# Gates and branch projections of a hybrid decoder layer: tokens as weights, 512 weight columns moving

## The chip, the cores and the metric

One core of a Trainium2 chip runs the whole layer in one launch. The metric is the device time of one execution in microseconds (us); less is better. TensorE (PE) multiplies matrices into PSUM, VectorE (DVE) and ScalarE (ACT) do the elementwise work, GpSimd (POOL) sets up masks and starts some DMAs, and the queue of SyncE (SP) starts nearly all DMAs.

## The reference

A residual layer over 256 tokens of width 2048 (one layer, batch 1):

```python
h = rms_norm(x, norm_w)
proj = h @ w_in                       # 2048 x 16592
(g_qkv, g_z, g_b, g_a, r_feat, r_z, s_u, s_z, gate_logits) = split(proj)
o_a = gdn_branch(...)                 # gated DeltaNet, width 1024
o_b = rwkv7_branch(...)               # RWKV-7 time mixing, width 1024
o_c = s5_branch(...)                  # diagonal SSM, GLU, times silu(s_z), width 1024
branch_proj = o_i @ w_branch[i]       # for o_a, o_b, o_c: 3 x (256 x 2048)
gates = sigmoid(gate_logits + gate_b) # 3 x (256 x 2048)
merged = sum(gates * branch_proj)
out = rms_norm(x + merged @ w_out, final_norm_w)
```

The three gates take 6144 of the 16592 columns of `w_in`. Everything is float32.

## The kernel before, in words

**Matmuls.** Each float32 product is made of three matmuls in the `float32r` type: both operands are split into a high and a low part, and high x high, high x low and low x high are added up in PSUM (names `whi`, `wlo` for weights, `hT`, `oT`, `mT` pairs for activations). `hT` is the normalised input turned, channels on partitions and 256 tokens in a row.

**Jobs and units.** The weights are read as a stream of units of 128 x 1024 numbers. `load_unit` issues the DMA (`raw`, 4 buffers), ACT makes `whi` (L267), DVE makes `wlo` (L268), 3 buffers each. `run_stream` loads two units ahead of the one that `mm_unit` multiplies. There are two sorts of job:

- `job_cols`: 128 weight columns are the stationary operand, the 256 tokens move. 16 steps (2048 channels) or 8 (1024), three matmuls of 128x256 each. The result has columns on partitions. A unit holds 8 steps.
- `job_tok`: 128 tokens are the stationary operand, up to 512 weight columns move. The result has tokens on partitions, one PSUM bank for each half of the tokens (`a` = 0, 1). A unit with 512 columns holds 2 steps, 12 matmuls. Before, only the output projection (`last`) used it.

**Order.** PE works in the order in which the program is written (class `InOrder`). The other engines are ordered by the scheduler of the framework, as tiles become ready. Other work is woven into the stream by hand: generators lie in lanes, and each call of `pump` is one turn; a generator that yields n is resumed n turns later. `mm_unit` calls `pump` after every second step of a `job_cols`, `run_stream` after every unit; so a turn is six matmuls, four turns a unit. `finish` runs lanes to their end.

**Stages.** 1: `front`, the inputs of DeltaNet and RWKV with their recurrences in lanes. 2: `front_gates`, six gate jobs (`NG` = 6 gate tiles are kept). 3: `front_su`, the input of S5. Then the right-hand pool `fp` closes, and `mp`, `s5p` and `sp` open on the right. 4: `back1`, the other 26 gate jobs of branches 0 and 1, their 32 projections, then six of the eight jobs of S5's gate (`sz_job`); S5 runs in lanes "s" and "sm" the while (`s5_setup`, `s5_mats`, `s5_tile`, eight tiles). The first step of `s5_setup` loads three parameters (`s5raw`, `s5ldt`), yields 1, and turns them on PE (tile `s5t`). 5: `back2`, two more `sz_job`, the GLU of S5, and gates and projections of branch 2. 6: `last`, the output projection and the final norm.

**Gate and projection before.** `gate_job(b, n)` makes 128 columns of gate b, `got_gate` applies tanh(x/2 + b/2) with the bias as ACT's per-partition operand (`hgate`). `proj_job(b, n)` makes the same 128 columns of a branch's projection from `oT[b]`; `got_proj` adds (tanh + 1) * projection to `merged` (columns on partitions, as the output projection wants it) and, with the third branch, splits it into `mT`. The PSUM pool `ps` has two banks for `mm` and six for `br` (everything else).

Of the kernel before, what the change touches and what calls it, by code (L numbers as in the profile page):

```python
# [18 lines left out]
P = 128  # L19
T = 256  # L20
# [16 lines left out]
def tile_trunk(  # L37
# [36 lines left out]
    st_o = ExitStack()  # L74
    op_ = st_o.enter_context(tc.tile_pool(name="op", bufs=1))
    dp = ctx.enter_context(tc.tile_pool(name="dp", bufs=2, space=bass.MemoryType.DRAM))
    ps = ctx.enter_context(tc.tile_pool(name="ps", bufs=1, space=PSUM))

    NB_MM, NB_BR = 2, 6

    def mm_bank(name):
        return ps.tile([P, 512], F32, tag="mm", bufs=NB_MM, name=name)

    def br_bank(name):
        return ps.tile([P, 512], F32, tag="br", bufs=NB_BR, name=name)
# [268 lines left out]

    gmask = cp.tile([P, 2, 64], F32, name="gmask")
    ge.memset(gmask, 1.0)

    lmask = cp.tile([P, 64], F32, name="lmask")
    ge.memset(lmask, 1.0)
    for h in range(2):  # L360
        sl = slice(64 * h, 64 * h + 64)
        select(gmask[sl, 0], ALU.is_gt, 0.0, 0, -1, [[1, 64]])
        select(gmask[sl, 1], ALU.is_ge, 0.0, 0, -1, [[1, 64]])
        select(lmask[sl], ALU.is_gt, 0.0, 0, 1, [[-1, 64]])
    ones = cp.tile([P, 1], F32, name="ones")
    ve.memset(ones, 1.0)
    blk2 = scr[:, 7, 0:P].rearrange("p (a b) -> p a b", a=2)
# [21 lines left out]
    for gi, g in enumerate(groups):  # L389
        rows, eng = pvr[gi], nc.sync  # L390
        if gi == 0:
            ge.memset(rows, 0.0)
        r0 = 0
        for name, src, n in g:
            if n == 0:
                eng.dma_start(out=rows[r0:r0 + 1, 0:96], in_=src.rearrange("(a c) -> a c", a=1))
                n = 1
            else:
                eng.dma_start(out=rows[r0:r0 + n, :], in_=src.rearrange("(a c) -> a c", c=P))
            pv_cols[name] = (gi, r0)  # L400
            r0 += n
        pvt.append((cp.tile([P, r0], F32, name=f"pv{gi}"), r0))

    def pv(name, i=0, n=1):
        gi, r0 = pv_cols[name]
# [6 lines left out]
    nkk = cp.tile([P, 8], F32, name="nkk")  # L412
    hw0 = cp.tile([P, 16], F32, name="hw0")
    hgb = cp.tile([P, 8], F32, name="hgb")
    hgate = cp.tile([P, 48], F32, name="hgate")
    hgnw = cp.tile([P, 1], F32, name="hgnw")
    hlw = cp.tile([P, 16], F32, name="hlw")
    hkk = cp.tile([P, 8], F32, name="hkk")
# [2 lines left out]
    ve.memset(cst[:, 0:1], -RW_C)  # L421
    ve.memset(cst[:, 1:2], EPS)

    def parameters():
        for gi, (t, n) in enumerate(pvt):
            pt = br_bank(f"pvps{gi}")
            pe.transpose(pt[:, 0:n], pvr[gi][:n], ident[:n, :n])
            ve.tensor_copy(t, pt[:, 0:n])
        ve.tensor_scalar(out=omu, in0=pv("mu", 0, 24), scalar1=-1.0, scalar2=1.0, op0=ALU.mult, op1=ALU.add)
        ve.tensor_scalar(out=omu2, in0=pv("mu_wl", 0, 2), scalar1=-1.0, scalar2=1.0, op0=ALU.mult, op1=ALU.add)  # L430
        ve.tensor_scalar(out=nkk, in0=pv("kk", 0, 8), scalar1=-1.0, scalar2=None, op0=ALU.mult)
        ve.tensor_scalar(out=oka, in0=pv("ka", 0, 8), scalar1=-0.5, scalar2=1.0, op0=ALU.mult, op1=ALU.add)
# [4 lines left out]
        ve.tensor_scalar(out=hgate, in0=pv("gate", 0, 48), scalar1=0.5, scalar2=None, op0=ALU.mult)  # L437
# [662 lines left out]
    def lane(name, gen):  # L1100
        lanes.setdefault(name, deque()).append(gen)
# [27 lines left out]
    def mm_unit(u):  # L1129
        job = u["job"]  # L1130
        if u["k0"] == 0:
            job["ps"] = [(br_bank if job["nps"] > 1 else mm_bank)(f"mm{un[0]}_{j}") for j in range(job["nps"])]
        kt, w, k0 = u["kt"], u["w"], u["k0"]
        last = k0 + kt == job["K"]
        mh, ml = job["mov"]()
        if job["tok"]:
# [5 lines left out]
            for a, v in todo:  # L1142
                o = job["ps"][a]
                for k in range(kt):
                    kk = v["k0"] + k
                    end = kk == job["K"] - 1
                    mhs, mls = mh[:, kk, a * P:(a + 1) * P], ml[:, kk, a * P:(a + 1) * P]
                    pe.matmul(o[:, 0:w], lhsT=mhs, rhs=v["hi"][:, k], start=kk == 0, stop=False)
                    pe.matmul(o[:, 0:w], lhsT=mhs, rhs=v["lo"][:, k], start=False, stop=False)
                    pe.matmul(o[:, 0:w], lhsT=mls, rhs=v["hi"][:, k], start=False, stop=end)  # L1150
                if end:
                    job["done"](a, o)
        else:
# [14 lines left out]
            if "after" in job:  # L1168
                job["after"]()

    def job_tok(mat, c, w, done, mov, late=False):
        job = {"K": KD, "tok": True, "nps": 2, "done": done, "mov": mov, "late": late}
        kt = UN // w
        for k0 in range(0, KD, kt):
# [61 lines left out]
    merged = []  # L1236
    gates = {}

    def got_gate(b, i):
        def f(pss):  # L1240
            t = gp.tile([P, T], F32, tag="gate", bufs=NG, name=f"gate{b}_{i}")
            se.activation(out=t, in_=pss[0][:, 0:T], func=AF.Tanh, scale=0.5, bias=hgate[:, b * 16 + i:b * 16 + i + 1])  # L1242
            gates[(b, i)] = t
        return f

    def got_proj(b, i):
        def f(pss):
            g, m, p0 = gates.pop((b, i)), merged[0][:, i], pss[0][:, 0:T]
            if b == 0:
                ve.scalar_tensor_tensor(out=m, in0=g, scalar=1.0, in1=p0, op0=ALU.add, op1=ALU.mult)  # L1250
                return
            ve.scalar_tensor_tensor(out=g, in0=g, scalar=1.0, in1=p0, op0=ALU.add, op1=ALU.mult)  # L1252
            ve.tensor_tensor(out=m, in0=m, in1=g, op=ALU.add)
            if b == 2:
                split(mT[0][:, i], mT[1][:, i], m)
        return f

    def gate_job(b, n):
        return job_cols(W, [(C_GATE + 2048 * b + P * n, P)], got_gate(b, n), hmov)

    def proj_job(b, n):
        return job_cols(w_branch[0, b], [(P * n, P)], got_proj(b, n), lambda: oT[b], K=8)

    NG = 6

    def front_gates():
        for i in range(NG):
            yield from gate_job(i % 2, i // 2)

    run_stream(front(), q=first)  # L1270
    run_stream(front_gates())
    finish("r")
    run_stream(front_su())
    finish("g", "r", "t", "i", "g2", "r2")
    fr.close()

    mp = ctx.enter_context(tc.tile_pool(name="mp", bufs=1, side="right"))
    merged.append(mp.tile([P, KD, T], F32, name="merged"))

    st_s5 = ExitStack()  # L1280
    s5p = st_s5.enter_context(tc.tile_pool(name="s5p", bufs=1, side="right"))
# [26 lines left out]
    def s5_setup(sp):  # L1308
# [2 lines left out]
        nc.sync.dma_start(out=raw[:, 1], in_=s5_a_im[0].rearrange("(i g) n -> i (g n)", g=2))  # L1311
        ldt = sp.tile([32, 2], F32, name="s5ldt")
        nc.sync.dma_start(out=ldt, in_=s5_log_dt[0].rearrange("(i g) -> i g", g=2))
        yield 1
        ve.tensor_copy(raw[:, 2].rearrange("p (g n) -> p g n", g=2), ldt.unsqueeze(2).to_broadcast([32, 2, 64]))
        pt = br_bank("s5t")
        for j in range(3):
# [295 lines left out]
            yield from s5_tile(t)  # L1613

    def back1():
        for n in range(16):
            for b in range(2):
                if (b, n) not in gates:
                    yield from gate_job(b, n)
                yield from proj_job(b, n)  # L1620

    sz = {}
    N_SZ = 6

    def got_sz(i):
        def f(pss):
            p0 = pss[0][:, 0:T]
            th = mp.tile([P, T], F32, tag="szt", name=f"szt{i}")
            se.activation(out=th, in_=p0, func=AF.Tanh, scale=0.5)
            if i < N_SZ // 2:  # L1630
                sz[i] = mp.tile([P, T], F32, tag="sz", bufs=N_SZ // 2, name=f"sz{i}")
            else:
                sz[i] = gp.tile([P, T], F32, tag="gate", bufs=NG, name=f"sz{i}")
            ve.scalar_tensor_tensor(out=sz[i], in0=th, scalar=1.0, in1=p0, op0=ALU.add, op1=ALU.mult)
        return f

    def sz_job(r):
        return job_cols(W, [(C_SZ + P * r, P)], got_sz(r), hmov)
# [121 lines left out]
```

## Time and profile before

| | |
|---|---|
| median of 3 runs | 1197.18 us (1196.2 to 1198.06) |
| the profiled execution | 1195.4 us, span 1193.6 us |
| granted TensorE clock, mean | 0.995 of full |
| busy: PE, PE's weight loads | 1168.8 us, 1128.4 us |
| busy: DVE, ACT, POOL | 905.6 us, 681.6 us, 56.2 us |
| HBM read, mean | 195.88 MB, 169 GB/s over the span |

The span runs from the first to the last instruction of the profiled execution; its time has 1.8 us around that. In the rows shown later, `out<-in` are the program's tile names, then the shapes; "xN | a, b | c" stands for N instructions, a us busy in all, b ns for one on average, c us of idle time of the engine just before them, followed by what ended that idle time. Rows of the timeline begin with the start in us and the length in us of a merged group. Matmuls overlap on PE, so the distance from start to start is their pace, and "mean ns of one" is longer. A row of the chain of waits gives start, length, engine, tile and line.

### The profile page before, as it was taken

Reading aid. Unit: us, or ns where it says so; the run is one execution under the profiler, and the core shown is the slowest. Engines: PE = TensorE matmul, PEld = TensorE weight load, DVE = VectorE, ACT = ScalarE, POOL = GpSimd, SP = SyncE. Lnnn points to the kernel's source line nnn. Section 1 sums busy time; section 2 is a strip of 40 time slices with the busy share of each in tenths; the row PEclk is TensorE's granted clock in tenths of the full one; section 3 lists DMA queues with packets and bytes.
Section 4 is the critical chain, followed back from the end, with each engine's and each line's share of the span. In section 5 each row is a group of like instructions: output and inputs, shape, how many; then the busy total and the mean of one; then the engine's idle time right before and its main releaser. Section 6 shows DMA issues by size and latency. Waiting matters only on the chain. (4 is left out here: it accounts for less than half of the span.)

```text
span 1193.6 us, 29078 instructions
## 1 busy us (share of the span) xinstructions
PE 1168.8 (98%) x11534; PEld 1128.4 (95%) x11534; DVE 905.6 (76%) x2261; ACT 681.6 (57%) x1412; POOL 56.2 (5%) x92
## 2 busy tenths in 40 slices
PE   7999999999999999999989999999999999999997
PEld 7999999999999999999989999999999999999887
DVE  7879696879787888885569979999986665555555
ACT  5465767676767776766534555555544544444443
POOL 1000000000000000000020111111000000000000
PEclk9999999999999999999989999999999999999999
DMA  7766555555656555555657677777776666667763
GB/s 203 195 180 171 153 139 148 141 149 147 159 130 158 148 141 131 132 149 144 182 157 191 181 189 188 195 190 191 185 185 169 182 189 179 188 183 239 242 197 116
DMA packets 384642, 203.97 MB, mean 171 GB/s; under 512 B 38825, under 2 KB 376186, under 8 KB 384122
## 3 DMA queue, kind: packets, MB, share of 16 engines
q1 hardware_dynamic: 382650, 199.61, 62.1%
q0 software_dynamic: 1536, 1.58, 0.6%
q8 instruction: 91, 1.49, 0.5%
q10 hardware_dynamic: 320, 0.93, 0.2%
q14 instruction: 45, 0.37, 0.1%
HBM read 195.88 MB, written 6.18 MB: 169 GB/s over the span
## 5 line engine op out<-in xcount | busy, mean ns | idle before, releaser
L62 PE MATMUL mm<-hT,whi 128*128 128x256 f32 (+1 forms) x4160 | 782.1, 288 | 0.0
L62 PEld LDWEIGHTS mm<-hT,whi 128*128 128x128 f32 (+1 forms) x4160 | 644.6, 191 | 7.3 <-issue 1.2
L62 PE MATMUL mm<-hT,wlo 128*128 128x256 f32 (+1 forms) x2080 | 587.4, 282 | 0.0
L268 DVE TENSOR_TENSOR wlo<-raw,whi 128x1024 fp32r<-128x1024 f32 (+1 forms) x346 | 422.3, 1221 | 184.7 <-ACT whi L267 181.6
L267 ACT ACTIVATE whi<-raw 128x1024 fp32r<-128x1024 f32 (+1 forms) x346 | 365.2, 1056 | 320.2 <-PE mm L62 239.3
L62 PEld LDWEIGHTS mm<-hT,wlo 128*128 128x128 f32 (+1 forms) x2080 | 396.4, 191 | 0.0
L62 PE MATMUL mm<-oT,whi 128*128 128x256 f32 x768 | 142.8, 286 | 0.0
L62 PEld LDWEIGHTS mm<-oT,whi 128*128 128x128 f32 x768 | 120.9, 194 | 0.5 <-issue 0.4
L62 PE MATMUL mm<-oT,wlo 128*128 128x256 f32 x384 | 109.3, 285 | 0.0
L62 PE MATMUL mm<-whi,mT 128*128 128x512 f32 (+1 forms) x288 | 76.8, 354 | 0.0
L62 PEld LDWEIGHTS mm<-oT,wlo 128*128 128x128 f32 x384 | 74.2, 193 | 0.0
L62 PEld LDWEIGHTS mm<-whi,mT 128*128 128x128 f32 x288 | 51.2, 189 | 7.5
L62 PE MATMUL mm<-wlo,mT 128*128 128x512 f32 (+1 forms) x144 | 50.9, 354 | 0.0
L570 DVE TENSOR_TENSOR ivp<-ivZ,ivX 48x1 f32<-48x1 f32 (+14 forms) x120 | 34.6, 288 | 2.0
L688 DVE SCALAR_TENSOR_TENSOR scr<-mm,pv,scr 128x255 f32<-128x255 f32 (+2 forms) x72 | 34.1, 473 | 0.6
L62 PEld LDWEIGHTS mm<-wlo,mT 128*128 128x128 f32 x144 | 27.2, 189 | 3.8
L572 DVE TENSOR_REDUCE ivZ<-ivp 48x1 f32<-48x1 f32 (+14 forms) x120 | 27.3, 227 | 1.7
L62 PE MATMUL mm<-ysp,whi 128*128 128x256 f32 x128 | 23.1, 283 | 0.0
L1252 DVE SCALAR_TENSOR_TENSOR gate<-gate,mm 128x256 f32<-128x256 f32 x32 | 13.3, 417 | 12.1 <-PE mm L62 11.9
L1242 ACT ACTIVATE gate<-mm,hgate 128x256 f32<-128x256 f32 x48 | 22.1, 461 | 0.3
L691 ACT ACTIVATE gth<-scr 128x256 f32<-128x256 f32 x24 | 9.9, 414 | 21.4 <-DVE scr L688 17.8
L62 PEld LDWEIGHTS mm<-ysp,whi 128*128 128x128 f32 x128 | 19.8, 189 | 0.0
(541 smaller groups left out, 1278.4 us busy)
## 6 DMA issues: line engine op xcount, KB each, us to landing
raw<-in_w_in_dram SPq DMA_DIRECT2D x256, 512.0 KB
raw<-in_w_branch_dram SPq DMA_DIRECT2D x48, 512.0 KB
raw<-in_w_out_dram SPq DMA_DIRECT2D x32, 512.0 KB
raw<-in_s_glu_w_dram SPq DMA_DIRECT2D x8, 512.0 KB
xs<-in_x_dram SPq DMA_DIRECT2D x4, 512.0 KB
xr<-in_x_dram SPq DMA_DIRECT2D x2, 1024.0 KB
raw<-in_w_in_dram SPq DMA_DIRECT2D x4, 384.0 KB
gr<-grow SPq DMA_DIRECT2D x8, 128.0 KB
```

What stands on the lines that cost most here:

```text
L62: return self.put(nc.tensor.matmul(*a, **k).ins)
L267: u["top"] = lambda: se.activation(out=hi[:, 0:nn], in_=raw[:, 0:nn], func=AF.Copy)
L268: u["sub"] = lambda eng=ve: eng.tensor_tensor(out=lo[:, 0:nn], in0=raw[:, 0:nn], in1=hi[:, 0:nn].bitcast(F32), op=ALU.subtract)
L570: ve.tensor_tensor(out=pi, in0=Z[:, 0:i, 0:i].rearrange("p j c -> p c j"), in1=X[:, i, 0:i].unsqueeze(1).to_broadcast([8 * NU, i, i]), op= ...
L572: ve.tensor_reduce(out=Z[:, i, 0:i], in_=pi, axis=AX.X, op=ALU.add)
L688: ve.scalar_tensor_tensor(out=c[:, s:T], in0=p[:, 0:T - s], scalar=pv("cw", (3 - s) * 24 + col), in1=c[:, s:T], op0=ALU.mult, op1=ALU.add)
L691: se.activation(out=th, in_=c, func=AF.Tanh, scale=0.5)
L1242: se.activation(out=t, in_=pss[0][:, 0:T], func=AF.Tanh, scale=0.5, bias=hgate[:, b * 16 + i:b * 16 + i + 1])
L1252: ve.scalar_tensor_tensor(out=g, in0=g, scalar=1.0, in1=p0, op0=ALU.add, op1=ALU.mult)
```

## The change

Gates and branch projections become `job_tok` jobs: 128 tokens stationary, 512 weight columns moving. 12 gate jobs instead of 48, 12 projections instead of 48. With that come:

- The gate's bias differs along the row now. It is split into a high and a low part at the start (`parameters`), written to DRAM (`bD`), and for each gate job loaded into rows 0, 1, 64 and 65 of a 128x512 tile that is otherwise zero (`brow`, two of them in turn, set to zero when `mp` opens). A matmul with `blk` (ones in the two diagonal blocks of 64x64) as weights starts each of the two banks with the bias.
- `merged` has tokens on partitions, 128 x 2 x 2048. A new lane "m" (`turn`) turns it with PE transposes after each projection of branch 2, two column blocks (four transposes) at a time, and splits the result into `mT`. What is left of the last one runs inside the first output job.
- Six `sz_job` go to the front in place of six gate jobs. `back1` is then gate and projection of branches 0 and 1 four times, one `sz_job` and the first gate of branch 2.
- `mm_unit` calls `pump` between the steps of a `job_tok` too, three times a unit of 512 columns; a turn is then three matmuls of 512.
- After the front the PSUM pool is closed and opened anew (`ps2`) with four `mm` banks and four `br` banks; `job_tok` takes `mm` banks.
- `s5_setup` yields 8 instead of 1 between its loads and the transposes of `s5t`.

```diff
@@ pools
+    st_ps = ExitStack()
+    banks = [st_ps.enter_context(tc.tile_pool(name="ps", bufs=1, space=PSUM)), 2]
     def mm_bank(name):
-        return ps.tile([P, 512], F32, tag="mm", bufs=NB_MM, name=name)
+        return banks[0].tile([P, 512], F32, tag="mm", bufs=banks[1], name=name)
     def br_bank(name):
-        return ps.tile([P, 512], F32, tag="br", bufs=NB_BR, name=name)
+        return banks[0].tile([P, 512], F32, tag="br", bufs=8 - banks[1], name=name)
...
+    bD = dp.tile([2, 3 * D], F32, tag="bD", bufs=1, name="bD")
     def parameters():
+        bh, bl = (sc3[0:48, (4 + e) * P:(5 + e) * P].bitcast(F32R) for e in range(2))
+        split(bh, bl, pvr[2][0:48])
+        for e, b in enumerate((bh, bl)):
+            nc.sync.dma_start(out=bD[e].rearrange("(a c) -> a c", c=P), in_=b.bitcast(F32))
...
@@ mm_unit
-            job["ps"] = [(br_bank if job["nps"] > 1 else mm_bank)(f"mm{un[0]}_{j}") for j in range(job["nps"])]
+            b_ = mm_bank if job["nps"] == 1 or job["tok"] else br_bank
+            job["ps"] = [b_(f"mm{un[0]}_{j}") for j in range(job["nps"])]
+            if "bias" in job:
+                for o in job["ps"]:
+                    pe.matmul(o, lhsT=blk, rhs=job["bias"].bitcast(F32R), start=True, stop=False)
...
+                    if "pre" in job and a == 0:
+                        job["pre"](kk)
-                    pe.matmul(o[:, 0:w], lhsT=mhs, rhs=v["hi"][:, k], start=kk == 0, stop=False)
+                    pe.matmul(o[:, 0:w], lhsT=mhs, rhs=v["hi"][:, k], start=kk == 0 and "bias" not in job, stop=False)
                     pe.matmul(o[:, 0:w], lhsT=mhs, rhs=v["lo"][:, k], start=False, stop=False)
                     pe.matmul(o[:, 0:w], lhsT=mls, rhs=v["hi"][:, k], start=False, stop=end)
+                    if not job["late"] and (a, k) != (1, kt - 1):
+                        pump()
...
+    NW = 512
+    brow = []
+    def got_gate(b, n):
+        gates[(b, n)] = mp.tile([P, 2, NW], F32, tag="gate", name=f"gate{b}_{n}")
+        def f(a, p):
+            se.activation(out=gates[(b, n)][:, a], in_=p, func=AF.Tanh, scale=0.5)
+        return f
+    def got_proj(b, n):
+        def f(a, p):
+            g, m = gates[(b, n)][:, a], merged[0][:, a, n * NW:(n + 1) * NW]
+            if b == 0:
+                ve.scalar_tensor_tensor(out=m, in0=g, scalar=1.0, in1=p, op0=ALU.add, op1=ALU.mult)
+                return
+            ve.scalar_tensor_tensor(out=g, in0=g, scalar=1.0, in1=p, op0=ALU.add, op1=ALU.mult)
+            ve.tensor_tensor(out=m, in0=m, in1=g, op=ALU.add)
+            if b == 2 and a:
+                lane("m", turn(n))
+        return f
+    def turn(n):
+        yield 4
+        for i in range(4 * n, 4 * n + 4, 2):
+            pt = br_bank(f"mt{i}")
+            for j in range(2):
+                for a in range(2):
+                    pe.transpose(pt[:, (2 * j + a) * P:(2 * j + a + 1) * P],
+                                 merged[0][:, a, (i + j) * P:(i + j + 1) * P], ident)
+            split(*(m[:, i:i + 2].rearrange("p k t -> p (k t)") for m in mT), pt)
+            yield 2
+    def gate_job(b, n):
+        t = brow[(4 * b + n) % 2]
+        for h in range(2):
+            nc.sync.dma_start(out=t[64 * h:64 * h + 2], in_=bD[:, b * D + n * NW:b * D + (n + 1) * NW])
+        return job_tok(W, C_GATE + D * b + NW * n, NW, got_gate(b, n), hmov, bias=t)
+    def proj_job(b, n):
+        return job_tok(w_branch[0, b], NW * n, NW, got_proj(b, n), lambda: oT[b], K=8)
...
     run_stream(front(), q=first)
-    run_stream(front_gates())
+    run_stream(front_sz())
     finish("r")
     run_stream(front_su())
     finish("g", "r", "t", "i", "g2", "r2")
     fr.close()
+    st_ps.close()
+    banks[:] = ctx.enter_context(tc.tile_pool(name="ps2", bufs=1, space=PSUM)), 4
     mp = ctx.enter_context(tc.tile_pool(name="mp", bufs=1, side="right"))
-    merged.append(mp.tile([P, KD, T], F32, name="merged"))
+    merged.append(mp.tile([P, 2, D], F32, name="merged"))
+    for i in range(2):
+        brow.append(mp.tile([P, NW], F32, name=f"brow{i}"))
+        ve.memset(brow[i], 0.0)
...
@@ s5_setup
-        yield 1
+        yield 8
...
     def back1():
-        for n in range(16):
+        for n in range(4):
             for b in range(2):
-                if (b, n) not in gates:
-                    yield from gate_job(b, n)
+                yield from gate_job(b, n)
                 yield from proj_job(b, n)
+        yield from sz_job(6)
+        yield from gate_job(2, 0)
...
     def back2():
-        for r in range(N_SZ, 8):
-            yield from sz_job(r)
+        yield from sz_job(7)
         for r in range(8):
             yield from job_cols(s5_glu_w[0], [(P * r, P)], got_glu(r), lambda: ysp, K=8)
-        for n in range(16):
-            yield from gate_job(2, n)
+        for n in range(4):
+            if n:
+                yield from gate_job(2, n)
             yield from proj_job(2, n)
...
     def last():
-            yield from job_tok(w_out[0], ocut[n], ocut[n + 1] - ocut[n], got_out(n), lambda: mT, late=n == NO - 1)
+            yield from job_tok(w_out[0], ocut[n], ocut[n + 1] - ocut[n], got_out(n), lambda: mT, late=n == NO - 1,
+                               **({} if n else {"pre": lambda k: k == 10 and finish("m")}))
```

More of the change, by code (lines that the diff above doesn't have):

```diff
@@ L76, in tile_trunk @@
     dp = ctx.enter_context(tc.tile_pool(name="dp", bufs=2, space=bass.MemoryType.DRAM))
-    ps = ctx.enter_context(tc.tile_pool(name="ps", bufs=1, space=PSUM))
-    NB_MM, NB_BR = 2, 6
+    st_ps = ExitStack()
+    banks = [st_ps.enter_context(tc.tile_pool(name="ps", bufs=1, space=PSUM)), 2]
     def mm_bank(name):
-        return ps.tile([P, 512], F32, tag="mm", bufs=NB_MM, name=name)
+        return banks[0].tile([P, 512], F32, tag="mm", bufs=banks[1], name=name)
     def br_bank(name):
-        return ps.tile([P, 512], F32, tag="br", bufs=NB_BR, name=name)
+        return banks[0].tile([P, 512], F32, tag="br", bufs=8 - banks[1], name=name)
     UN = 1024
@@ L356, in tile_trunk @@
     ge.memset(gmask, 1.0)
-    lmask = cp.tile([P, 64], F32, name="lmask")
-    ge.memset(lmask, 1.0)
     for h in range(2):
@@ L363, in tile_trunk @@
         select(gmask[sl, 1], ALU.is_ge, 0.0, 0, -1, [[1, 64]])
-        select(lmask[sl], ALU.is_gt, 0.0, 0, 1, [[-1, 64]])
     ones = cp.tile([P, 1], F32, name="ones")
@@ L401, in tile_trunk @@
             r0 += n
-        pvt.append((cp.tile([P, r0], F32, name=f"pv{gi}"), r0))
+        if gi < 2:
+            pvt.append((cp.tile([P, r0], F32, name=f"pv{gi}"), r0))
     def pv(name, i=0, n=1):
@@ L414, in tile_trunk @@
     hgb = cp.tile([P, 8], F32, name="hgb")
-    hgate = cp.tile([P, 48], F32, name="hgate")
     hgnw = cp.tile([P, 1], F32, name="hgnw")
@@ L436, in parameters @@
         ve.tensor_scalar(out=hgb, in0=pv("gb", 0, 8), scalar1=0.5, scalar2=None, op0=ALU.mult)
-        ve.tensor_scalar(out=hgate, in0=pv("gate", 0, 48), scalar1=0.5, scalar2=None, op0=ALU.mult)
         ve.tensor_scalar(out=hgnw, in0=pv("gnw"), scalar1=0.5, scalar2=None, op0=ALU.mult)
@@ L1169, in mm_unit, with job_tok @@
                 job["after"]()
-    def job_tok(mat, c, w, done, mov, late=False):
-        job = {"K": KD, "tok": True, "nps": 2, "done": done, "mov": mov, "late": late}
+    def job_tok(mat, c, w, done, mov, late=False, K=KD, **more):
+        job = {"K": K, "tok": True, "nps": 2, "done": done, "mov": mov, "late": late, **more}
         kt = UN // w
-        for k0 in range(0, KD, kt):
+        for k0 in range(0, K, kt):
             u = {"job": job, "k0": k0, "kt": kt, "w": w, "src": [(0, w, mat[k0 * P:(k0 + kt) * P, c:c + w])]}
@@ L1237, in tile_trunk @@
     gates = {}
-    def got_gate(b, i):
-        def f(pss):
-            t = gp.tile([P, T], F32, tag="gate", bufs=NG, name=f"gate{b}_{i}")
-            se.activation(out=t, in_=pss[0][:, 0:T], func=AF.Tanh, scale=0.5, bias=hgate[:, b * 16 + i:b * 16 + i + 1])
-            gates[(b, i)] = t
-        return f
[L1246 to L1268, printed above, removed]
+    NW = 512
[5 more added lines that the diff above has]
+        return f
@@ new lines, in proj_job, with got_sz @@
+    def proj_job(b, n):
+        return job_tok(w_branch[0, b], NW * n, NW, got_proj(b, n), lambda: oT[b], K=8)
+    sz = {}
+    N_SZ = 6
+    def got_sz(i):
+        def f(pss):
+            p0 = pss[0][:, 0:T]
+            th = ft([P, T], "gth", f"szt{i}") if i < N_SZ else mp.tile([P, T], F32, tag="szt", name=f"szt{i}")
+            se.activation(out=th, in_=p0, func=AF.Tanh, scale=0.5)
+            if i < N_SZ:
+                sz[i] = gp.tile([P, T], F32, name=f"sz{i}")
+            else:
+                sz[i] = mp.tile([P, T], F32, name=f"sz{i}")
+            ve.scalar_tensor_tensor(out=sz[i], in0=th, scalar=1.0, in1=p0, op0=ALU.add, op1=ALU.mult)
+        return f
@@ L1270, in tile_trunk, with sz_job, front_sz @@
+    def sz_job(r):
+        return job_cols(W, [(C_SZ + P * r, P)], got_sz(r), hmov)
+    def front_sz():
+        for i in range(N_SZ):
+            yield from sz_job(i)
     run_stream(front(), q=first)
-    run_stream(front_gates())
+    run_stream(front_sz())
     finish("r")
@@ L1615, in back1 @@
     def back1():
-        for n in range(16):
+        for n in range(4):
             for b in range(2):
-                if (b, n) not in gates:
-                    yield from gate_job(b, n)
+                yield from gate_job(b, n)
                 yield from proj_job(b, n)
[L1622 to L1638, printed above, removed]
+        yield from sz_job(6)
+        yield from gate_job(2, 0)
     lane("s", s5_all())
     run_stream(back1())
-    run_stream(job for r in range(N_SZ) for job in sz_job(r))
     finish("s", "sm")
```

## The prediction

> **What bounds the kernel now.** I read the page first, then the chain of waits, the groups of instructions, and the timeline where the chain has a hole.
>
> ```profile
> PE 1168.8 (98%) x11534; PEld 1128.4 (95%) x11534; DVE 905.6 (76%) x2261; ACT 681.6 (57%) x1412; POOL 56.2 (5%) x92
> ...
> PEclk9999999999999999999989999999999999999999
> ```
>
> PE is busy for 98% of the span and its granted clock dips in one slice alone, the 21st (597 to 627 us). In the chain, in order of time, I looked for what is not PE's matmuls:
>
> ```profile
> 617.21 0.69 PE s5t L65 x3
> 617.89 57.28 PE mm L62 x456
> 675.18 0.44 PE s5bt L65 x4
> ...
> 676.55 15.11 PE mm L62 x126
> ```
>
> It is S5's few transposes, and the hole ahead of s5t, which the dip of the clock goes with. So the time follows the number of PE instructions times their pace, plus that hole. The pace with 256 moving columns is 15.11 us / 126 = 119.9 ns a matmul.
>
> ```profile
> L62 PE MATMUL mm<-hT,wlo 128*128 128x256 f32 x2048 | 578.4, 282 | 0.0
> L62 PE MATMUL mm<-oT,wlo 128*128 128x256 f32 x384 | 109.3, 285 | 0.0
> 1100.59 0.61 PE L62 MATMUL mm<-whi,mT 128*128 128x512 f32 x2
> ...
> 1134.59 0.61 PE L62 MATMUL mm<-whi,mT 128*128 128x512 f32 x2
> ```
>
> The first two rows (groups by form) give the counts: 2048 low-part matmuls are 128 jobs of 16, 384 are 48 jobs of 8, and each step has three matmuls. The last two (timeline) are the output projection, which already has tokens as weights and 512 columns moving. Between them lie 50 triples (each two whi matmuls and one wlo): 34.00 us / 150 = 226.7 ns. Two matmuls of 256 cost 239.8 ns, one of 512 costs 226.7: about 13 ns per instruction do not scale with the columns, and they are what the change can save.
>
> **Pace.** Gates: 48 jobs x 16 x 3 = 2304 matmuls; projections: 48 x 8 x 3 = 1152. Together 3456 x 119.9 ns = 414.4 us. After: the same columns in 1728 matmuls of 512 (12 gate jobs of 96, 12 projections of 48), 391.7 us at the pace of the output projection, whose operands have the same kinds and shapes. Gain 22.7 us. All of it is on PE's path.
>
> **Bias by a matmul.** Two more matmuls of 512 for each of 12 gate jobs: 24 x 226.7 ns = 5.4 us added on PE. The ACT bias operand that they replace cost PE nothing.
>
> **Turning the merged sum.** 32 transposes of 128x128. The row of s5bt has four such in 0.44 us, so 32 x 0.11 = 3.5 us added. The columns' splits become eight of 512 on ACT and DVE, in stages where neither is full.
>
> Sum on PE: -22.7 + 5.4 + 3.5 = -13.8 us.
>
> The Trainium skill, "TensorE: Matmul & The Clock Gate", section "Back-to-back issue gap", gives an isolated matmul N/2.4 + 2.5 ns at full clock, so only some 2.5 ns that halving the count could save: 1728 x 2.5 = 4.3 us, less than 24 x 215.8 ns for the biases and 32 x 55.8 ns for the turns (7.0 us), a loss of 2.7 us for these parts by an estimate from that page. The trace does not agree: 119.9 and 226.7 ns here, where it would give 109.2 and 215.8.
>
> **The hole at the change of stage.** Here the change says that S5's set-up turns later. The timeline around it, all engines:
>
> ```profile
> 595.50 3.47 SPq L264 DMA_DIRECT2D raw<-in_w_branch_dram  x2
> ...
> 612.34 0.40 PE L62 MATMUL mm<-oT,whi 128*128 128x256 f32 x2
> ...
> 613.41 0.43 DVE L105 TENSOR_TENSOR oT<-rog,oT 128x256 fp32r<-128x256 f32 x1 [0.48 <-ACT oT L104]
> 614.00 0.09 DVE L1419 MEMSET cb<- 128x32 f32 x1 [0.16 <-DVE oT L105]
> 614.04 0.31 POOL L1296 MEMSET B<- 128x256 f32 x1 [107.05 <-DVE oT L105]
> 614.12 0.37 SPq L1310 DMA_DIRECT2D s5raw<-in_s_a_re_dram  x1
> 615.01 0.45 SPq L1313 DMA_DIRECT2D s5ldt<-in_s_log_dt_dram  x1
> ...
> 617.21 0.69 PE L65 MATMUL s5t<-ident,s5raw 32*128 32x32 f32 x3 [3.99 <-DMA uD<-us]
> 617.31 0.22 DVE L1315 COPY s5raw<-s5ldt 32x128 f32<-32x128 f32 x1 [1.46 <-DMA s5ldt<-in_s_log_dt_dram]
> ...
> 618.63 0.63 PE L62 MATMUL mm<-oT,whi 128*128 128x256 f32 x2
> ...
> 622.47 0.55 PE L62 MATMUL mm<-oT,whi 128*128 128x256 f32 x2
> ...
> L548 DVE MEMSET Mr<- 128x512 f32 x2 | 1.0, 485 | 0.1
> ```
>
> DVE, POOL and SP all first touch the tiles of the new pools between 614.00 and 614.12, right after the last reader of the old right-hand pool (613.41 + 0.43). So whatever lies in a pool opened there waits until 614.0. PE ran six matmuls of the first projection, then stood at s5t, whose loads were issued at 614.12 to 615.01 and were there at 617.2 (2.3 us from the issue of s5ldt to the copy that waited for it). Lost: 617.89 - 612.34, less six matmuls (0.72) and three transposes at full speed (0.33), is 4.5 us. After it PE is slow: from 618.63 to 622.47 six triples take 3.84 us, 213 ns a matmul; against 119.9 that loses 2.1 us from 617.89 to 622.47. Hole and after-effect cost 6.6 us.
>
> The change lets seven turns pass ahead of s5t, 21 matmuls or 4.8 us: s5t no longer waits. But the stage now begins with a gate, and the first instruction of a gate is the bias matmul. It reads brow, a tile in mp, which opens at the same 614.0. Ahead of it lie a memset of 128x512 (485 ns), then two loads on SP's queue, 0.43 us apart, then the 2.3 us. If they go first: 614.0 + 0.5 + 0.45 + 2.3 = 617.3. If SP has s5's two or three loads out first, because those need no memset, up to 618.1. PE has nothing else: its order is fixed, and every matmul of the stage is queued behind the bias. It stops at 612.34 and loses 5.0 to 5.8 us; I take 5.4, 0.9 more than before. The new PSUM pool also has to wait, for the last copy out of the old banks, which ends sooner and so is under it. The slow 5 us after it remain. Ends: -6.6 (no wait left) and +1.3.
>
> The same page of the Trainium skill, section "HAM oscillation", has a gap of PE over about 3.4 us put the array back to half clock. The 3.99 us hole and the 213 ns agree; by it the new hole would have to fall under 3.4 us before the 2.1 us came back.
>
> **DVE in the S5 stage.**
>
> ```profile
> 500.00:600.00 100.00, 98.83 (x1055) 95.31 (x1055) 63.93 (x163) 62.27 (x151) 1.22 (x1) 1.00 0.57 149
> 727.25:754.50 27.25, 27.25 (x326) 26.55 (x326) 25.61 (x57) 13.79 (x28) 3.65 (x6) 1.00 0.69 182
> ...
> 743.17 0.42 DVE L1581 TENSOR_TENSOR s5s<-s5m,s5m 128x256 f32<-128x256 f32 x1
> 745.23 0.97 PE L62 MATMUL s5y<-s5s,CX 128*32 128x64 f32 x56
> ...
> L1253 DVE TENSOR_TENSOR merged<-merged,gate 128x256 f32<-128x256 f32 x32 | 13.5, 421 | 0.7
> L1702 DVE SCALAR_TENSOR_TENSOR xr<-mm,xr 128x512 f32<-128x512 f32 x6 | 3.8, 682 | 0.0
> L268 DVE TENSOR_TENSOR wlo<-raw,whi 128x1024 fp32r<-128x1024 f32 x342 | 418.2, 1224 | 184.7 <-ACT whi L267 181.6 <-DMA UM<-uD 0.6
> ```
>
> The second row is one S5 tile (columns: stretch, its length, busy PE, PEld, DVE, ACT, POOL, clock, DMA): 33 turns of six matmuls, DVE busy 25.61 of 27.25 us. A turn shrinks from 0.72 to 0.68 us, so a tile to 25.9 us. The merge of two branches falls from 12 instructions of 0.42 per 512 columns to 6 of 0.68; a tile's 198 matmuls are 1.4 of four such column blocks, so that takes 0.3 us off it: DVE 25.3 of 25.9. It fits, barely. The tightest spot is s5s to s5y: done at 743.59, used at 745.23, 1.6 us spare. From s5u to s5y are 21 turns, so 0.84 is lost. The merge now comes in lumps: a projection of the second branch ends in 4 x 0.68 = 2.7 us of DVE at once, every 96 turns. Counted in turns, two of the eight tiles have such a lump inside this stretch (3 x 0.42 before): late by 0.84 + 1.5 - 1.6 = 0.7 us each. I take +0.7 in all, with ends 0 and 5.4 (all eight). The four br banks hold s5bt, two s5u and s5ct at once, just enough. S5 then ends at turn 372 of 424 instead of 365 of 384, well covered.
>
> **The turn's own wait.** The transposes come three turns, nine matmuls or 2.0 us, after the last matmul of proj(2,n). DVE needs two instructions of 0.68 after that; a split of 1.22 in between makes them late by up to 0.7. Four times: 0 to 2.8, I take 0.7. The last turn lies under the first output job, which needs its columns only at the twelfth of 16 steps.
>
> **At nothing.** Six S5-gate jobs for six merge-gate jobs in front: same matmuls, and DVE has room there (64% from 500 to 600 us, first row above). Each gate's two brow loads go to SP ahead of that gate's weights; they wait for a bias matmul two gates back, long done, so they hold up neither the weights nor S5's loads behind them. The first projection's weights were issued at 595.50 for 612.34, so such loads have 17 us of lead; without it each would cost up to 2.3 us. The bD writes, brow's repeated loads and 2 KB instead of 512-byte rows are under PE. The start loses a transpose and gains a small split: 0 to 0.5.
>
> **Sum.** -13.8 + 0.9 + 0.7 + 0.7 = -11.5 us. The profiled execution took 1195.4 us (span 1193.6), so 1183.9; the median of the runs, 1197.18, stands 1.8 above it: 1185.7.
>
> **The rivals.**
> *The hole closes too.* If brow were not held up by the old pool, 4.5 + 2.1 us come back: 1197.2 - 13.8 - 6.6 + 1.4 = 1178.2. Against it: three engines that start at 614.0 together.
> *DVE late, in part.* All eight tiles late by 0.7 and every turn late: 1197.2 - 13.8 + 0.9 + 5.4 + 2.8 = 1192.5.
> *DVE becomes the bound (the other side).* Place: s5s ahead of s5y. If three more splits of 1.22 stand in front of the last s5s in each tile, s5y is late by 3.7 + 0.84 - 1.6 = 2.9 us, eight times: 1197.2 - 13.8 + 0.9 + 0.7 + 23 = 1208. It decides from 1.8 us a tile on (14 us over eight). For it: 94% busy in that tile's row. Against it: DVE's total falls.
> *The pace does not come.* If a 512 matmul costs two of 256 in these stages, -11.5 + 22.7: 1208. Against it: 50 even triples at 226.7. The gap rule of the Trainium skill, weighed above, speaks for a milder form of it.
> *Bias late at every gate.* Eleven more waits of up to 2.3 us: 1211. Against it: the lead of 17 us.
>
> **Chances.** Forecast 0.62 (own range 1182 to 1189). Hole closed 0.13. DVE late in part 0.11. DVE the bound 0.09, of which 0.04 ends within 0.2%. Pace 0.02, bias 0.03. About 0.2%, 2.4 us, is what a measurement of this kernel can tell. Faster 0.86, same 0.04, slower 0.10. The range 1178 to 1191.5 reaches to the closed hole and most of the partial case, leaving out some 2 in 10.
>
> **What will show it.** mm<-whi,hT and mm<-whi,oT of 512 at 680 ns a triple; 24 matmuls reading brow and blk; the first of them with 4.5 to 6 us of idle time before it, released by a DMA, and triples near twice the time after it; s5t without a wait; gaps ahead of s5y of under 1 us in two tiles and ahead of mt of under 1 us. It is wrong if no idle time stands before the first bias, if s5y waits in every tile, or if the triples are slower than 0.70.

## The result, and the profile after

The changed kernel takes 1187.74 us (median of 4 runs, 1186.22 to 1189.48), the kernel before beside it 1196.69 (4 runs): ratio 0.9929, 95% interval 0.9913 to 0.9944, 9.0 us faster. The forecast was 1185.7. The profiled execution is the slowest of the four, 1189.48 us.

The head of its page:

```profile
span 1187.6 us, 25599 instructions
...
PE 1160.4 (98%) x9861; PEld 1045.8 (88%) x9861; DVE 898.2 (76%) x2214; ACT 674.9 (57%) x1381; POOL 55.6 (5%) x89
...
PEclk9999999999999999999999999999999999999998
```

PE is still the bound. It has 1673 instructions fewer (11534 before), and loading weights leaves room: 88% of the span, not 95%. Next the groups by form, the matmuls that are new here:

```profile
L62 PE MATMUL mm<-whi,hT 128*128 128x512 f32 x768 | 246.7, 395 | 0.0
L62 PE MATMUL mm<-wlo,hT 128*128 128x512 f32 x384 | 150.8, 393 | 0.6 <-DVE wlo L267 0.5
...
L62 PE MATMUL mm<-brow,blk 128*128 128x512 f32 x24 | 8.0, 415 | 3.9 <-DMA s5raw<-in_s_a_im_dram 3.9
...
L65 PE MATMUL mt<-ident,merged 128*128 128x128 f32 x32 | 4.9, 274 | 0.0
```

The 24 bias matmuls hold the stage's one large idle time, and the 32 transposes of the merged sum have none ahead of them. The timeline of all engines at the change of stage, where the hole of the kernel before was:

```profile
615.02 0.28 PE L62 MATMUL mm<-hT,wlo 128*128 128x256 f32 x1
...
615.84 0.42 DVE L104 TENSOR_TENSOR oT<-rog,oT 128x256 fp32r<-128x256 f32 x1 [0.48 <-ACT oT L103]
...
616.50 1.02 DVE L1327 MEMSET brow<- 128x512 f32 x2 [0.24 <-DVE oT L104]
616.54 0.37 SPq L1359 DMA_DIRECT2D s5raw<-in_s_a_re_dram  x1
...
617.02 0.55 SPq L1285 DMA_DIRECT2D brow<-bD  x2
...
619.16 1.19 PE L62 MATMUL mm<-brow,blk 128*128 128x512 f32 x2 [3.86 <-DMA s5raw<-in_s_a_im_dram]
...
621.00 1.05 PE L62 MATMUL mm<-whi,hT 128*128 128x512 f32 x2
...
622.28 1.06 PE L62 MATMUL mm<-whi,hT 128*128 128x512 f32 x2
...
626.40 0.62 PE L62 MATMUL mm<-whi,hT 128*128 128x512 f32 x2
...
627.08 0.62 PE L62 MATMUL mm<-whi,hT 128*128 128x512 f32 x2
...
628.08 0.37 PE L65 MATMUL s5t<-ident,s5raw 32*128 32x32 f32 x3
```

Front's last matmul starts at 615.02 and is over at 615.14, counted at its pace of 0.12 us; PE stands until 619.16, 4.0 us. Then a triple takes 1.28 us (621.00 to 622.28; the granted clock from 620 to 625 is 0.50), and 0.68 from about 625 on. 22 matmuls from 619.16 to 627.08 take 7.92 us, at 226.7 ns they would take 4.99: 2.9 lost. So the hole costs 6.9 us, and s5t stands in it no more: no idle time ahead of it at 628.08. The profile puts the wait down to the DMA that landed last, s5raw, which the bias matmul doesn't read; brow's loads went out between those of s5raw.

In S5's stage, the chain of waits (first and last s5y) and the windows:

```profile
721.68 1.47 PE s5y L62 x72
...
908.76 1.47 PE s5y L62 x72
```

```profile
700.00:800.00 100.00, 98.89 (x797) 79.45 (x796) 90.67 (x186) 52.67 (x103) 13.06 (x22) 1.00 0.65 187
800.00:900.00 100.00, 99.57 (x875) 79.68 (x874) 91.96 (x195) 49.03 (x92) 7.28 (x12) 1.00 0.67 194
```

```profile
PE s5y L62 <- DVE s5s L1629: 0.9, 2, 0.6
...
PE mm L62 <- DVE wlo L267: 0.5, 1, 0.5
```

The waits (PE rows: in total, times, longest) are for DVE's results, but the idle time that they show is only part of the loss. Seven tile periods are 187.08 us, 26.73 each. They hold 703 matmuls of 512, 159.4 us at 226.7 ns, so that 27.7 are left for S5's own PE work and for waits. The same seven periods of the kernel before are 190.2 us with 1386 matmuls of 256, 166.2 at 119.9 ns, and 24.0 are left. S5's work is the same, so 3.7 us are lost here: 1.8 at the two late s5y, 0.9 at two late weight splits, and 1.0 in small pieces, none over 0.15 us.

The times of one kernel's runs spread by up to 5 us, and the traces point to front. Front hardly differs between these kernels, but its last matmul starts at 615.02 in this trace, at 612.0 to 614.3 in the others. Behind it, the traces of different kernels agree to 0.06 us, matmul by matmul, for as long as their code is the same, which is 100 us at the most. So I compare the time **behind front** too: the span's end less the end of front's last matmul (its start and 0.12 us). Each kernel has one trace, so how much this time varies between runs of one kernel isn't known. Before 1193.6 - 612.34 = 581.3, after 1187.6 - 615.14 = 572.5: 8.8 less, as the medians say.

### The profile page after: what moved, and what is told of

Read it like the earlier page. It is cut to its first block, busy times and chain, and to the rows that moved or that the text cites. A ratio compares the mean times of both kernels' runs of the same rounds, so it can differ in the third digit from the quotient of the medians.

```text
span 1187.6 us, 25599 instructions
## 1 busy us (share of the span) xinstructions
PE 1160.4 (98%) x9861; PEld 1045.8 (88%) x9861; DVE 898.2 (76%) x2214; ACT 674.9 (57%) x1381; POOL 55.6 (5%) x89
## 4 chain that ended last, share of the span: by engine, by line
PE 84%; DVE 7%; DMA 4%; ACT 3%; issue 1%; SPq 0%; DVEq 0%; ACTq 0%
PE mm L62 74%; DVE wlo L267 2%; DMA rD<-rL 1%; PE s5y L62 1%; DMA ivX<-rD 1%; ACT whi L266 1%; DVE ivp L571 1%; DMA xs<-in_x_dram 1%; PE ryo L62 1%; DVE scr L689 0%; DVE ivZ L573 0%; PE rg L62 0%; DMA ivT<-zD 0%; PE warm L65 0%; PE gg L62 0%
## 5 line engine op out<-in xcount | busy, mean ns | idle before, releaser
L62 PE MATMUL mm<-hT,whi 128*128 128x256 f32 (+2 forms) x2624 | 503.5, 291 | 0.0
L62 PEld LDWEIGHTS mm<-hT,whi 128*128 128x128 f32 (+2 forms) x2624 | 407.5, 191 | 5.9
L62 PE MATMUL mm<-hT,wlo 128*128 128x256 f32 (+2 forms) x1312 | 371.0, 283 | 0.0
L62 PEld LDWEIGHTS mm<-hT,wlo 128*128 128x128 f32 (+2 forms) x1312 | 250.2, 191 | 0.0
L62 PE MATMUL mm<-whi,hT 128*128 128x512 f32 x768 | 246.7, 395 | 0.0
L62 PEld LDWEIGHTS mm<-whi,hT 128*128 128x128 f32 x768 | 145.5, 189 | 31.1 <-issue 1.2
L62 PE MATMUL mm<-wlo,hT 128*128 128x512 f32 x384 | 150.8, 393 | 0.6 <-DVE wlo L267 0.5
L62 PE MATMUL mm<-whi,oT 128*128 128x512 f32 x384 | 122.6, 392 | 0.0
L62 PEld LDWEIGHTS mm<-wlo,hT 128*128 128x128 f32 x384 | 72.7, 189 | 16.0 <-DVE wlo L267 1.4
L62 PE MATMUL mm<-wlo,oT 128*128 128x512 f32 x192 | 74.8, 390 | 0.0
```

What stands on the lines that cost most here:

```text
L62: return self.put(nc.tensor.matmul(*a, **k).ins)
```

## The experiments

The theory: the gain is the pace; a wait for brow has taken the place of the wait for s5t; and some microseconds are lost to DVE in S5's stage. The rivals stand in each expectation. Ratios are to the kernel before, on the same chip.

**1. The bias last, and left out.** In mm_unit:

```
-            if "bias" in job:
-                for o in job["ps"]:
-                    pe.matmul(o, lhsT=blk, rhs=job["bias"].bitcast(F32R), start=True, stop=False)
...
                 if end:
+                    if "bias" in job:
+                        pe.matmul(o, lhsT=blk, rhs=job["bias"].bitcast(F32R), start=False, stop=True)
                     job["done"](a, o)
```

> The changed kernel with one difference: a gate's two bias matmuls come after its last step instead of ahead of its first. Theory A (the hole at the change of stage is the first bias matmul's wait for brow; it costs 4.0 us of idle PE and 2.9 us of slow matmuls behind it): PE starts the first gate when the last copy out of the old banks is done (616.1 in the changed kernel's trace, 1.0 us after the last front matmul), loses perhaps 1 us more on the third weights, and keeps its clock: 4.5 to 6 us less than the changed kernel's 1187.7, so 1182 to 1183. Rival (the new pools as such hold the stage up, the PSUM pool or the queue of loads, and brow only comes last by chance): PE starts at 618 to 619 all the same, with slow triples behind it, and the time stays within 1 us of 1187.7.

1183.55 us, ratio 0.9893 (0.9876 to 0.9910), half a microsecond over the range; behind front 568.4. The timeline of PE:

```profile
614.27 0.28 PE L62 MATMUL mm<-hT,wlo 128*128 128x256 f32 x1
615.39 0.50 PE L62 MATMUL mm<-whi,hT 128*128 128x512 f32 x1 [0.83 <-ACT us L1090]
```

The gate starts when the last copy out of the old banks is done, 1.0 us after front, at full clock, and no weights are late there. So brow was the wait, and the hole shrinks from 6.9 us to 1.0. But the time behind front falls by 4.1 only: 1.8 of the 5.9 come back. Of these, 1.0 lie in S5's seven periods (188.05 us with the same 703 matmuls), where the waits for wlo are now 1.5 us instead of 0.5, and 0.5 at the transposes of the merged sum.

The other run leaves out the gates' bias: no brow, no loads of it, no bias matmuls.

> The changed kernel without the gates' bias: no brow, no loads of it, no bias matmuls (the gates' bias is left out). Theory A: the hole shrinks as in the run with the bias last, and 24 x 226.7 ns = 5.4 us of PE work go: 5 to 5.5 us under that run, 10 to 11.5 under the changed kernel, 1176 to 1178. Rival (PE waits for DVE's weight splits and S5 in this stage anyway, so that work taken from PE comes back as waits): no more than 2 us under the run with the bias last.

1177.85 us, ratio 0.9845 (0.9828 to 0.9862); behind front 562.8, 5.6 under the bias last. The bias costs its 24 x 226.7 ns in full; PE work taken away here is time gained.

**2. The pace.** 256 moving columns, all else kept (`NW = 256`, and what follows from it):

> The changed kernel with 256 instead of 512 moving columns in gates and projections, tokens still as weights, everything else kept. Theory A (the gain is the pace, 13 ns for every matmul saved): 3456 matmuls at 119.9 ns instead of 1728 at 226.7 are 22.7 us more, the biases 0.3 more: 1209 to 1212. Rival (the gain comes from elsewhere, the merge in fewer and longer instructions or the other order of the stage): under 5 us more, up to 1193.

1261.52 us, ratio 1.0543 (1.0526 to 1.0561): the theory missed it by 50 us, the rival by more. A wait and a window of that run:

```profile
PE s5y L62 <- DVE s5s L1629: 23.6, 7, 4.1
```

```profile
700.00:800.00 100.00, 79.35 (x1030) 72.48 (x1031) 92.17 (x222) 39.90 (x99) 14.56 (x24) 0.91 0.46 127
```

I had overlooked that S5's work is dealt out by turns, and a turn is one triple here: with 256 columns 0.36 us instead of 0.68. S5 asks DVE for the same work in half the time; PE then waits, and loses its clock (0.91). The repeat deals a turn after every second triple:

```
-                    if not job["late"] and (a, k) != (1, kt - 1):
+                    if not job["late"] and (w == 512 or k % 2) and (a, k) != (1, kt - 1):
```

> The kernel with 256 moving columns again, with S5's lanes pumped after every second triple, so that a turn of S5 lasts 0.72 us as with 512 columns (0.68) and not 0.36. Theory A (the 13 ns for each matmul are the gain; the run with 256 columns lost the other 50 us because S5's turns came twice as fast as DVE can follow): 1209 to 1212, hardly any wait of s5y for s5s. Rival (tokens as weights with 256 columns cost more by themselves, in weight splits or merges that DVE can't keep up with): 1225 or more.

1206.13 us, ratio 1.0081 (1.0066 to 1.0096); behind front 591.4, 19.0 over the changed kernel. The pace accounts for 23.0 (22.7, and 0.3 for 48 bias matmuls of 119.9 ns instead of 24 of 226.7). So 4.0 were won, and the time is 2.9 us under the theory's range. The window and the group by form show where:

```profile
700.00:800.00 100.00, 100.00 (x1153) 97.68 (x1152) 88.99 (x189) 51.33 (x104) 13.07 (x22) 1.00 0.66 185
```

```profile
L62 PE MATMUL s5y<-s5s,CX 128*32 128x64 f32 x512 | 8.6, 218 | 0.0
```

PE is busy throughout this window and has no idle time ahead of s5y in any tile; the seven periods have 24.1 us beside their matmuls, where the kernel before has 24.0. That is 3.7 of the 4.0; two others nearly cancel: the wait for brow is 4.0 us as well, but the slow matmuls behind it cost 1.6 instead of 2.9, and near 978 us PE loses 1.5 in waits for the third branch's oT. So the 512 columns win 22.7 us, and 3.7 go back in S5's stage, where DVE is late. Whether that is the turns, 6% shorter with 512 columns, or the merge's lumps, twice as long, this run doesn't tell apart. It does bound the parts of the change that have no run of their own (the jobs in front, the PSUM banks, the order of the stage): it takes 10.1 us more than the kernel before behind front, and biases (5.8), turning (3.5), the wait for oT (1.5) and the smaller hole (-1.1) make 9.7.

**3. S5's set-up turns later.** This part alone on the kernel before (`yield 1` to `yield 8`):

> The kernel before with one part of the change alone: S5's set-up yields 8 turns instead of 1 ahead of its transposes. Theory A: the hole ahead of s5t (4.5 us of idle PE, 2.1 us of slow matmuls) goes, nothing waits in its place, and S5 has turns to spare at its end: 5 to 6.6 us under the kernel before, 1190 to 1192, ratio 0.9945 to 0.996. Rival (something else of the new stage is late next, the third weights behind S5's loads on SP's queue): 2 us or less, ratio over 0.998.

1189.84 us, ratio 0.9945 (0.9930 to 0.9960). Behind front 574.5, 6.7 less:

```profile
619.01 0.28 PE L62 MATMUL mm<-oT,wlo 128*128 128x256 f32 x1
619.23 0.37 PE L65 MATMUL s5t<-ident,s5raw 32*128 32x32 f32 x3
```

No idle time and no slow matmuls are left: the whole hole of the kernel before, 4.5 + 2.1, was in those seven turns. So this one number in the kernel before wins 6.7 us where the whole change wins 8.8, and the two intervals overlap. Then the part undone in the changed kernel:

> The changed kernel with S5's set-up back at 1 turn instead of 8. Theory A (in the changed kernel the wait for brow stands ahead of s5t and covers its loads, so this part of the change brings nothing here): within 1.5 us of 1187.7, s5t with under 1 us of idle time. Rival (the turns are what closed the hole of the kernel before, and brow added one of its own): a second wait at s5t and 3 us more or beyond, 1190.5 or higher.

1185.86 us, ratio 0.9913 (0.9898 to 0.9928), which overlaps the changed kernel's; 0.3 us beyond the bound, on the side away from the rival; behind front 571.4, 1.1 less. s5t starts at 619.88 without idle time, under the wait for brow. The turns bring nothing there. And undone with the bias last:

> The kernel with the bias last (1183.55), with S5's set-up at 1 turn instead of 8. Theory A (with brow out of the way the next wait is s5t's, for loads that are issued at 615.8 to 618.4 and land 2.3 us later): PE stands 3.5 to 4.5 us ahead of s5t and may lose 2 us more of clock, 1187 to 1190. Rival (the turns have no price of their own): under 1 us, up to 1184.5.

1189.20 us, ratio 0.9941 (0.9924 to 0.9958), behind front 574.2, 5.8 more than with the turns. PE's timeline, and the clock of the windows (the number behind POOL's):

```profile
617.04 0.52 PE L65 MATMUL s5t<-ident,s5raw 32*128 32x32 f32 x2 [2.08 <-DMA s5raw<-in_s_a_im_dram]
617.85 0.31 PE L65 MATMUL s5t<-ident,s5raw 32*128 32x32 f32 x1 [0.29 <-DVE s5raw L1364]
```

```profile
615.00:620.00 5.00, 2.66 (x8) 2.06 (x9) 3.54 (x15) 0.00 (x0) 4.96 (x9) 0.68 0.64 187
620.00:625.00 5.00, 5.00 (x16) 3.97 (x15) 3.47 (x17) 1.06 (x1) 1.99 (x4) 0.64 0.18 44
```

The idle time ahead of s5t is shorter than I expected, 2.4 us, and the clock is lost all the same, so that the hole is nearly as dear as before. In the changed kernel the later turns and the later bias each leave a hole; only together do they close it.

**4. DVE in S5's stage.** Five runs try to win back what the bias-last kernel still waits (1.5 us for wlo, 0.9 for s5s by the profile); none did. The first puts the second branch's adds on GpSimd:

```
-            ve.tensor_tensor(out=m, in0=m, in1=g, op=ALU.add)
+            (ge if b == 1 else ve).tensor_tensor(out=m, in0=m, in1=g, op=ALU.add)
```

> The kernel with the bias last (1183.55), with the second branch's eight merge adds (m = m + g, 128x512) on GpSimd instead of VectorE. Theory A (the 3.5 us that PE still waits in S5's stage, for wlo at 761 and 841 us and for s5s at 769 and 850 us, are DVE's lumps after a projection of the second branch): DVE gets 5.4 us back in four places, the four waits fall under 1.5 us in all, 1181 to 1182.5. Rival (the adds are not what makes DVE late there, or GpSimd's adds slow DVE down): no less than 1183, the same four waits.

1185.56 us, ratio 0.9911 (0.9896 to 0.9926), behind front 570.5, 2.1 more. The timeline of DVE and POOL, and what PE does after it:

```profile
757.18 1.41 POOL L1265 TENSOR_TENSOR merged<-merged,gate 128x512 f32<-128x512 f32 x1 [3.40 <-DVE gate L1264]
757.35 2.32 DVE L267 TENSOR_TENSOR wlo<-raw,whi 128x1024 fp32r<-128x1024 f32 x1
...
761.08 1.22 DVE L267 TENSOR_TENSOR wlo<-raw,whi 128x1024 fp32r<-128x1024 f32 x1
761.24 2.21 POOL L1265 TENSOR_TENSOR merged<-merged,gate 128x512 f32<-128x512 f32 x1 [2.65 <-DVE gate L1264]
762.21 1.52 DVE L1617 TENSOR_TENSOR s5m<-s5m,s5m 128x256 f32<-128x256 f32 x1
...
769.10 2.02 PE L62 MATMUL s5y<-s5s,CX 128*32 128x64 f32 x64 [1.71 <-DVE s5s L1629]
```

The split takes 2.32 us instead of 1.22, about as much longer as the add had still to run; s5m takes 1.52 instead of 0.42. An add costs DVE 0.68 when it does it itself and, in these two rows, 1.1 when GpSimd does it (0.5 to 1.1 over the eight adds). By the Trainium skill, "SBUF — State Buffer", section "SBUF: two separate sides", VectorE and GpSimd share one port pair as an exclusive lock, which whichever starts first holds for its whole instruction, where a VectorE instruction has two SBUF inputs; the rows agree, and in the other direction too: the add took 1.41 us in the first row, 2.21 in the second, where it began behind a split.

But some 1.5 of the 2.1 us are the clock. From the late s5y to the sixth matmul of weights behind it PE takes 4.5 us, 3.0 with the bias last. The window of this run, then of the bias last:

```profile
770.00:775.00 5.00, 5.00 (x71) 4.06 (x62) 4.72 (x15) 1.91 (x8) 1.53 (x2) 0.71 0.57 151
```

```profile
770.00:775.00 5.00, 4.80 (x94) 3.88 (x95) 5.00 (x14) 1.79 (x4) 0.70 (x1) 1.00 0.66 185
```

So the adds on GpSimd relieve nothing, but how much they cost by themselves this run doesn't show.

Seven turns instead of four between s5s and s5y:

> The kernel with the bias last (1183.55), with seven turns instead of four between S5's s5s and its s5y. Theory A (PE waits for s5s in two of eight tiles, 1.0 and 0.7 us beyond its pace, because a projection of the second branch ends inside that stretch; three turns are 2.0 us, and S5 ends 24 turns later, which the stage has): both waits go, 1 to 2 us less, 1181.5 to 1182.5. Rival (DVE's backlog then shows at the next place, the weight splits): the same time within 0.7 us, more waits for wlo.

1189.27 us, ratio 0.9941 (0.9929 to 0.9953), behind front 575.6. The two waits are gone; a new one stands at the end:

```profile
942.60 2.06 PE L62 MATMUL s5y<-s5s,CX 128*32 128x64 f32 x64 [4.39 <-DVE s5s L1629]
```

The next tile but one is prepared when a look, taken every 35 turns, finds a tile finished. Three turns more make it miss such looks (twice, by the s5y of this trace: 51 us between tiles instead of 26 to 29); S5 then outlasts the stage's weights, and its last tile runs with nothing beside it.

A fourth pair of weight buffers, three units ahead:

> The kernel with the bias last (1183.55), with a fourth pair of weight buffers once S5's set-up is over, so that three units of weights are loaded and split ahead instead of two. Theory A (DVE is short for moments only, 93% busy from 700 to 800 us, and more lead evens out its lumps): the two waits for wlo (1.1 and 0.7 us beyond the pace) go, those for s5s stay, 1181.5 to 1183. Rival (DVE is short as such, and splits made earlier stand in front of S5's own instructions): longer waits for s5s, 1184 or more.

1185.31 us, ratio 0.9908 (0.9892 to 0.9923), behind front 571.7, 3.3 more. The time is the rival's.

```profile
PE s5y L62 <- DVE s5s L1632: 2.7, 2, 1.7
```

The wait for wlo is gone, that for s5s three times as long. At the first late tile PE comes 0.5 us earlier than with the bias last and s5s 0.6 later, both counted from front's end; which of DVE's instructions makes it later is not shown. The clock is lost here too (0.66 from 770 to 775 us). Both edits together:

> Both of these: seven turns ahead of s5y and the fourth pair of weight buffers. Theory A: the four waits of S5's stage (3.5 us beyond the pace with the bias last) all go, 1180 to 1181.5. Rival (they only change places): 1183 or more.

1189.39 us, ratio 0.9947 (0.9934 to 0.9960), behind front 574.4: the end of S5 again, 3.3 us ahead of the last s5y. Last, two turns more, which miss no look:

> The kernel with the bias last (1183.55), with six turns instead of four between s5s and s5y: two turns more (1.36 us), not three. With three the preparation of the next tile but one missed its look at the finished tile, which comes every 35 turns, in three places, and S5 ended after the stage's weights; counted in turns, two keep every tile at 33 turns and S5's end at turn 374 of 424. Theory A (the two waits for s5s, 0.6 and 0.3 us of idle PE and 1.7 us beyond its pace, are a matter of 0.6 us and cost what they show): they go and nothing else moves, 1181.5 to 1183. Rival (DVE's backlog comes back at the weight splits or the next tile): the same time within 0.7 us, 1183 to 1184.3, with longer waits for wlo.

1185.03 us, ratio 0.9916 (0.9903 to 0.9930), beyond both ranges; behind front 569.3: 0.9 more than the bias last, though no s5y waits. PE with the bias last (s5y and s5wt side by side), then with two turns more (apart):

```profile
715.11 0.64 PE L62 MATMUL s5y<-UM,WT 128*32 128x256 f32 x8
...
717.02 0.50 PE L62 MATMUL mm<-whi,oT 128*128 128x512 f32 x1
```

```profile
712.93 0.64 PE L62 MATMUL s5wt<-CX,B 128*32 128x128 f32 x16
713.51 0.50 PE L62 MATMUL mm<-whi,oT 128*128 128x512 f32 x1
...
715.11 0.64 PE L62 MATMUL s5y<-UM,WT 128*32 128x256 f32 x8
...
716.58 0.50 PE L62 MATMUL mm<-whi,oT 128*128 128x512 f32 x1
```

1.91 us for both groups side by side, 0.58 + 1.47 = 2.05 apart: 0.14 in each of seven tiles, 1.0 in all, and the waits for wlo grow by 0.2. That is 1.2 of what has to make up for the lost waits; the rest I can't name. The intervals of this run, of the adds on GpSimd and of the fourth buffers overlap that of the bias last, so what they lose rests on one trace each; none of them is faster, by its median or its trace.

The fastest version that has the bias is the bias last, 1183.55 us. It beats the changed kernel, whose interval (0.9913 to 0.9944) lies above its own (0.9876 to 0.9910).

## Why the prediction was right, and where it was off

Predicted -11.5 us, measured -8.8 behind front and -9.0 by the medians.

- **Pace, -22.7.** Right: 0.68 us a triple in both stages, and the repeat with 256 columns shows the 23.0 once its 4.0 is set beside it. The Trainium skill's section "Back-to-back issue gap" gives its 2.5 ns for an isolated matmul, and these are streams with a weight load ahead of each; the loss of 2.7 us that the prediction estimated from it did not come.
- **Bias, +5.4.** Right: 5.6 behind front when it is left out.
- **Turning, +3.5, and its wait, +0.7.** 32 transposes came to 3.0, and no idle time stands ahead of them. Four transposes, by PE's timeline:

```profile
990.02 0.60 PE L65 MATMUL mt<-ident,merged 128*128 128x128 f32 x4
990.37 0.48 PE L62 MATMUL mm<-whi,hT 128*128 128x512 f32 x1
990.69 0.39 PE L62 MATMUL mm<-wlo,hT 128*128 128x512 f32 x1
```

  0.35 us for four (0.51 in one group of the eight). The matmul behind them takes 0.32 us instead of 0.23, eight times, another 0.7: 3.7 in all. The order of DVE's work had no split between the merge and the transposes.
- **The hole, +0.9.** The mechanism was right in each part: the bias matmul waits for brow, s5t waits no more, the slow clock remains. Lost were 4.0 us, not 5.0 to 5.8: the new pools opened 1.4 us after front (616.50), not 1.7, and from there to the first bias matmul passed 2.7 us, not 3.3 to 4.1. The slow part was 2.9, not 2.1. 6.9 against 6.7 before: +0.2. That the size came so near is partly luck. The prediction took the slow part as it was before; behind the same idle time of 4.0 us it cost 2.9 here and 1.6 in the repeat with 256 columns, where the granted clock was low for half as long.
- **DVE in S5's stage, +0.7.** This is the step that was mis-sized: 3.7 were lost in the seven periods. I counted two late s5y at 0.7 us each, which is 1.4, and took half of it without a reason (all eight would be 5.6, not 5.4). Those two came, and cost 1.8. What I left out is that the weight splits come late behind a lump too (0.9), and 1.0 of small losses whose cause isn't shown. The repeat with 256 columns and longer turns gives the 3.7 back. The time lies between the forecast and the rival "DVE late, in part" at 1192.5, without that rival's late turns.
- **The sum.** -22.7 + 5.4 + 3.7 + 0.2 + 3.7 = -9.7; the 0.9 to -8.8 is spread over the paces and is not traced. The forecast was too dear at the hole and the turning by 1.2 us and too cheap at DVE by 3.0, so that a part of its nearness is that these go opposite ways.
- **The rivals.** "The hole closes too" needed brow out of the way, as run 1 made it; at 1183.55 it stays above that rival's 1178.2, because DVE takes part of it back. DVE did not become the bound, the pace came, and no other bias was late.

## What to carry to other kernels

When a change makes the bound engine's unit of work shorter, ask which other work is dealt out in that unit: here S5's turns became 6% shorter, and 3.7 of the 22.7 us won on PE were lost again in that stage, 2.7 of them at late results of VectorE. When a wait is moved away, put the first instruction of the next stage on data that are there already, and add the rest of its inputs last: the bias at the end of its sum instead of its start gave 4 us for nothing. With VectorE 91% busy there, none of the attempts to move its work in time or elsewhere won anything. And try the smallest part of a change alone: one number in S5's set-up gave the kernel before 6.7 us.

## What the runs showed of the hardware that I had not expected

In the run with the bias last and the turns early, PE stood three times within 4.9 us, for 0.83, 2.08 and 0.29 us, and lost the clock inside the second gap (0.90 granted from 616 to 617 us, 0.50 from 617 to 618). The Trainium skill, "TensorE: Matmul & The Clock Gate", section "HAM oscillation", names gaps over about 3.4 us; no single gap here was that long. The gap of 0.83 us alone, in the bias-last run, did not cost it. Nor does the length of a gap decide it: 1.71 us behind one of 0.60 cost the clock in the run with the adds on GpSimd (0.71 from 770 to 775 us), and 1.71 us behind one of 0.70 did not, later in the run with the turns early (at 850.54; 1.00 from 850 to 855 us).

GpSimd adds of 1.41 and 2.21 us each lengthened the VectorE instruction that began beside them by 1.10 us, in the rows shown. And behind front, traces agree to 0.06 us or better up to the first difference of code, so that a trace may tell 1 us where the medians can't; but the run with seven turns ahead of s5y is 5.7 us over the bias last by the medians and 7.2 by the traces, so the trace of one run is no proof of the last microsecond either.
